# A gated delta rule inside a hybrid decoder trunk: the decay's running sums along the row, read from DRAM on every partition instead of made by broadcast products

## The chip, the core and the metric

The kernel runs on one core of one Trainium2 chip. The metric is the device time of one execution in microseconds (us), and the time of a kernel is the median over its runs. Beside the times there is one profiled execution, in which the hardware profiler records each instruction of the core's engines: PE is TensorE (matrix products, PEld its weight loads), DVE is VectorE, ACT is ScalarE, POOL is GpSimd, and SP issues DMAs. L121 means line 121 of the kernel. Each engine takes its own instructions strictly in the order in which they stand in its program; between engines they wait for one another by semaphores.

## What is computed

Two layers of a decoder trunk on 1024 tokens with model width 1024, all in float32. A layer normalises its input, makes one wide input projection from it, runs three token mixers side by side (a gated delta rule with 4 heads of width 128, latent attention with 8 heads, and a linear recurrence, RG-LRU, 512 wide), and adds one output projection to its input. The change lies in the delta rule, which works on chunks of 64 tokens:

```python
gc = jnp.cumsum(g.reshape(B, N, C, H).transpose(0, 1, 3, 2), axis=-1)   # g: log decay
decay = jnp.exp(jnp.where(tril, gc[..., :, None] - gc[..., None, :], -jnp.inf))
kbeta = kc * bc
a_mat = jnp.where(strict, jnp.einsum('bnhid,bnhjd->bnhij', kbeta, kc) * decay, 0.0) \
    + jnp.eye(C, dtype=q.dtype)
rhs = jnp.concatenate([vc * bc, kbeta * jnp.exp(gc)[..., None]], axis=-1)
sol = lax.linalg.triangular_solve(a_mat, rhs, left_side=True, lower=True, unit_diagonal=True)
attn = jnp.where(tril, jnp.einsum('bnhid,bnhjd->bnhij', qc, kc) * decay, 0.0)
```

For each chunk and head, `decay[i, j]` is the exponential of gc of token i minus gc of token j. One of the two varies down the partitions of a tile and can be a scalar per partition; the other varies along the row and must be there on every partition. This second one is what the change is about.

## The kernel before

**Tiling.** Tokens are taken in 8 units of 128 (two chunks each), and heads in two pairs. A quad is 2 units by 2 heads of a pair, that is four 128x128 blocks side by side in one tile of 128x512. There are four quads to a pair and 16 in the whole program (4 quads, 2 pairs, 2 layers).

**The stage around the change.** `phase_a` runs once a layer:

1. `gates` makes the log decay g [128 tokens, 32 columns (unit, head)], and from it with small products (L247, L249) the running sums `gs` by token, and their totals by chunk.
2. `gdn_qkv` makes q, k and v of pair 0.
3. For each pair: `gdn_tok` transposes k and v to rows of tokens (copies ktok and vtok), takes the squared norms of k by 16 squares on ACT into the tile sk (the squares themselves go to junk, L86), and from them rk (Ln, then Exp, with a table load before each), and on DVE the factors br and nbr2 and others.
4. `gdn_pre` for the four quads, the function that is changed. For each quad: products of the broadcast column of g with the constant upper triangle (L347, four of them) put the running sums along the row into a PSUM bank on every partition; DVE subtracts the per-token sums from them and adds a mask, for ea and et, four instructions each; ACT takes their exponentials; the k product (L360, four) gives k k^T, from which DVE makes a with nbr2 and ea, which goes to DRAM (L364); the q product (L367, four) gives k q^T, from which DVE makes at with et.
5. `gdn_inverse` for the pair, then `gdn_prep` and `gdn_scan` for each quad, then `gdn_norm`.

After both pairs come the RG-LRU, the output projection and the attention (`phase_c`).

**What fills in.** The input projection is made one column tile of 128 columns at a time: `in_tile` makes each in three float32r products per block of 128 rows (`mm3`, L121 to L123), into the PSUM tile pbig. `load_w` gets the weights: DMA to wst (L104), a rounded part whi by DVE (L111), the rest wlo by POOL (L112). Column tiles that the delta rule does not need itself are placed between its steps: one after `gdn_tok`, and in pair 0 another after each quad of `gdn_pre`.

**What sets the order.** A scheduler lays out each engine's instructions once, when the program is made, by priority and its expected durations. Projections have a much lower priority, by `LOW`, so a projection is placed where the scheduler expects PE to have nothing else that is ready. On the chip nothing is reordered.

**Buffers.** `bank("pr")` is a PSUM tag with two banks, taken in turn by the transposes, the products of L347, L360 and L367 and others; a product that takes a bank must wait until the earlier content was read. The tile ea has one buffer, et has one, a two, at four.

Of the kernel before, what the change touches and what calls it, by code (L numbers as in the profile page):

```python
# [15 lines left out]
T = 1024  # L16
# [6 lines left out]
# Columns of a layer's parameter tile [128, NPAR].  # L23
# [15 lines left out]
# Columns of the constant tile [128, NCON].  # L39
# [10 lines left out]
# Indices of the input projection's column tiles.  # L50
# [13 lines left out]
class Trunk:  # L64
# [7 lines left out]
    @contextmanager  # L72
    def prio(self, d):
        """Instructions that the scheduler prefers less (d > 0) or more (d < 0)."""
        self.tc.cur_priority += d
        yield
        self.tc.cur_priority -= d
# [19 lines left out]
    def load_w(self, src, nk, cols, eng=None, pool=None):  # L97
        """A float32 weight block [128, nk, cols] as its exact float32r parts."""
        nc = self.nc
        n = nk * cols  # L100
        wn = self.wn if pool is None else n
        pool = pool or self.pw
        st = pool.tile([128, wn], F32, name="wst", tag="wst")
        nc.sync.dma_start(st[:, :n], src.rearrange("p k c -> p (k c)"))  # L104
        hi = pool.tile([128, wn], F32R, name="whi", tag="whi")
        lo = pool.tile([128, wn], F32R, name="wlo", tag="wlo")
        with self.prio(-self.LOW):
            if wn <= 512:
                nc.scalar.copy(hi[:, :n], st[:, :n])  # L109
            else:  # L110
                nc.vector.tensor_copy(hi[:, :n], st[:, :n])  # L111
            (eng or nc.gpsimd).tensor_tensor(lo[:, :n], st[:, :n], hi[:, :n].bitcast(F32), ALU.subtract)  # L112
        return (hi[:, :n].rearrange("p (k c) -> p k c", k=nk),
                lo[:, :n].rearrange("p (k c) -> p k c", k=nk))

    def mm3(self, out, pairs):
        """out = sum over (ah, al, bh, bl) of a.T @ b, each in three float32r products."""
        nc = self.nc
        n = len(pairs)
        for j, (ah, al, bh, bl) in enumerate(pairs):  # L120
            nc.tensor.matmul(out, ah, bh, start=(j == 0), stop=False)  # L121
            nc.tensor.matmul(out, ah, bl, start=False, stop=False)  # L122
            nc.tensor.matmul(out, al, bh, start=False, stop=(j == n - 1))  # L123

    def split(self, hi, lo, x, eng=None):
        """x as exact float32r parts: hi is x rounded, lo the rest."""
        self.nc.scalar.copy(hi, x)  # L127
        (eng or self.nc.vector).tensor_tensor(lo, x, hi.bitcast(F32), ALU.subtract)  # L128

# [1 line left out]
    def in_tile(self, l, *ms):  # L131
        """The first of the column tiles ms; the others wait for their call. All by halves of the tokens."""
        if ms[0] not in self.ready:
            tiles = []
            for m in ms:
                hi, lo = self.early.pop(m, None) or self.load_w(self.i["w_in"][l, m], 8, 128)
                self.ready[m] = self.big()
                tiles.append((hi, lo, self.ready[m]))
            with self.prio(self.LOW):
                for n in range(2):  # L140
                    s = slice(n * H2, (n + 1) * H2)
                    for hi, lo, p in tiles:
                        self.mm3(p[:, s], [(hi[:, k], lo[:, k], self.hh[k][:, s], self.hl[k][:, s]) for k in range(8)])
        return self.ready.pop(ms[0])

    def conv(self, y, p, w, bias=None):
        """Causal depthwise conv of width 4 along the free axis, from PSUM."""
        if bias is None:
            self.act(y, p, AF.Copy, scale=w[:, 3:4])
        else:  # L150
            self.act(y, p, AF.Identity, scale=w[:, 3:4], bias=bias)
        for d in (1, 2, 3):
            self.stt(y[:, d:], p[:, : T - d], w[:, 3 - d : 4 - d], y[:, d:], ALU.mult, ALU.add)

    def silu2(self, out, z):
        """out = 2 silu(z), as z (1 + tanh(z / 2))."""
# [7 lines left out]
    def newton(self, r, x):  # L164
        """One Newton step of r towards x ** -0.5; x is overwritten."""
# [5 lines left out]
    def add_squares(self, alloc, acc, x, eng):  # L171
        """acc + x * x (acc is None at first)"""
# [7 lines left out]
    def rms_bcast(self, alloc, accs, n, ch, tag, fine=False):  # L180
        """1 / sqrt(mean of squares + eps), on every partition, from the sum of accs over their channels."""
        nc = self.nc
        r = alloc("rb")
        if not fine:
            # brings Ln's table in while the sums are still under way
            self.act(self.dummy, accs[-1][:, 0:1], AF.Ln, bias=self.eps)
# [14 lines left out]
    def norm_half(self, alloc, xs, accs, n, gain, tag, share=False):  # L201
        """h = rmsnorm(x) for one half of the tokens, into self.hh, self.hl."""
# [12 lines left out]
    def gates(self, l):  # L215
# [16 lines left out]
        # beside them the RG-LRU's parameters  # L232
# [15 lines left out]
        for j, c in ((1, K_H0), (2, K_H1)):  # L248
            nc.tensor.matmul(pc[:, 32 * j : 32 * j + 32], con[:, c : c + 1].to_broadcast([128, 128]), gf, start=True, stop=True)  # L249
        gs = pa.tile([128, 96], F32, name="gs")  # L250
# [19 lines left out]
    def gdn_qkv(self, l, pr, kind, hd, P):  # L270
# [22 lines left out]
        # squared norms of q, columns (unit, head)  # L293
# [7 lines left out]
    def combos(self, q):  # L301
        """The four (unit, head) of quad q: index, unit, head of the pair, columns."""
        return [(c, 2 * q + c // 2, c % 2, slice(c * 128, c * 128 + 128)) for c in range(4)]

    def gdn_tok(self, pr, P):
        """k and v by token, and the pair's factors per token."""
# [14 lines left out]
        # inverse norms: 1 / sqrt(sum + eps), of vectors that are twice the reference's  # L321
# [9 lines left out]
        # v is held doubled  # L331
# [7 lines left out]
    def gdn_pre(self, pr, P, q):  # L339
        """-A and the decayed attention of one quad; the diagonal blocks go out by DRAM."""  # L340
# [3 lines left out]
        pg = self.bank("pr")  # L344
        for c, u, hd, cs in self.combos(q):
            gj = u * 4 + 2 * pr + hd
            nc.tensor.matmul(pg[:, cs], self.g[:, gj : gj + 1].to_broadcast([128, 128]),  # L347
                             con[:, K_U : K_U + 128], start=True, stop=True)
# [23 lines left out]
    def blocks(self, dram, b):  # L372
        """Diagonal block b (32 x 32) of each of a pair's sixteen 128 x 128 matrices."""
        return bass.AP(dram.tensor, dram.offset + b * (32 * 2048 + 32), [[128, 16], [2048, 32], [1, 32]])

    def gdn_inverse(self, pr):
        """(I + A)^-1 of the 32 x 32 diagonal blocks, one block per partition, and its transpose."""
# [18 lines left out]
    def gdn_prep(self, pr, P, q):  # L396
        """The quad's triangular inverse, applied to v and k."""
# [29 lines left out]
        for hd in range(2):  # L427
            # w of a unit's two chunks around that unit's q
# [10 lines left out]
    def gdn_scan(self, pr, P, q):  # L439
# [6 lines left out]
        # the output takes the place of the decayed attention  # L446
# [30 lines left out]
    def gdn_norm(self, pr, P):  # L477
        """The output's RMS norm, its gate and its way out; q's inverse norm and 128^-0.5 with them."""
# [31 lines left out]
    def gate_tile(self, l, m, dst, z=None):  # L510
        """2 silu of a column tile, to DRAM"""
# [7 lines left out]
    def lru(self, l):  # L519
        nc, pa, par = self.nc, self.pa, self.par  # L520
        st, res = [], []
        for m in range(4):
# [22 lines left out]
            # 1 - a^2 = tanh(-log a) (1 + a^2)  # L545
# [112 lines left out]
    def rope(self, x, n, s):  # L658
        """Rotary embedding of one half of the tokens; x may be in PSUM."""
# [13 lines left out]
    def attn_q_rope(self, l, pr, res):  # L673
        """q's rotary part of two heads: parts stacked as [hi; lo] per head."""
# [30 lines left out]
    def attn_v(self, l, pr, V):  # L705
        """v of two heads: per two token blocks, [128, (block, head, 128)]."""
# [16 lines left out]
    def attn_scores(self, h, sb, q, qr, k, P):  # L723
        """The normalised probabilities of four query blocks."""
# [3 lines left out]
        for qi in range(4):  # L728
# [3 lines left out]
            # pieces of the keys, a PSUM bank each  # L732
# [34 lines left out]
            if qi == 3:  # L767
                # the transposes wait for the last block's first keys
# [9 lines left out]
    def attn_out(self, h, sb, P, V, ops):  # L778
        """Probabilities times v, gated; transposed a block of keys ahead of the product."""
# [56 lines left out]
    def out_proj_last(self, wsrc, ops, xin, xout, alloc):  # L836
        """The same by halves, with the sums kept on chip; yields each half's tiles and sums of squares."""
# [28 lines left out]
    def build(self):  # L866
# [5 lines left out]
        with sb("pk") as pk, sb("pg") as self.pg, sb("pf", 2) as self.pf, sb("ph", 16) as self.ph, \  # L872
# [14 lines left out]
            self.krd = dr("krd", 64)  # L887
            self.dz = [dr(f"dz{p}", 128, 2048) for p in range(2)]
# [23 lines left out]
    def first_norm(self, p0):  # L912
        """Loads x and the constants; the first layer's normalised input."""
# [92 lines left out]
    def phase_c(self, l, xd):  # L1006
# [19 lines left out]
        # Pieces of work by the time of their emission; a step is a head's half of the queries.  # L1026
# [85 lines left out]
def kblocks(w, nk, cols):  # L1112
    """[L, nk * 128, M * cols] as [L, M, 128, nk, cols]"""
# [63 lines left out]
```

## Time and profile before

| What | before |
| --- | --- |
| median of 3 runs | 2239.93 us (2239.56, 2239.93, 2247.45) |
| profiled execution, from its first to its last instruction (its span; no other time of it is given) | 2240.5 us |
| instructions in it | 28710 |
| bytes moved by DMA | 222.06 MB, 99 GB/s on the mean |
| the four stretches with `gdn_pre` | 136.9 to 162.2, 333.3 to 357.4, 1236.8 to 1262.0, 1437.6 to 1463.0 us |
| granted TensorE clock, mean of the span and in these four | 0.984; 1.00, 1.00, 1.00, 0.93 |

How to read it: a share of busy time is an average over stages with different limits. In a list by time a row has the start in us, the duration in us, the engine, the line, the operation, and "out<-in" by the names of the tiles, then partitions x elements; xN is the number of records, and what stands in square brackets is how long the engine was idle before it and what it waited for. One float32 128x128 product is two records. Matrix products run pipelined, so that the next one starts before the recorded end of the one ahead; the step from start to start is what one costs. The granted clock is the share of TensorE's full speed that the chip's throttle grants at that time.

### The profile page before, as it was taken

To read this page: it belongs to the slowest core of one execution; us is meant where nothing else is said; L and a number is where in the kernel's file an instruction comes from. 1 tells how busy PE (TensorE), PEld (TensorE's weight loads), DVE (VectorE), ACT (ScalarE), POOL (GpSimd) and SP (SyncE) were. 2 spreads that over 40 slices of the span, in tenths; PEclk is the share of its full clock that TensorE was granted. 3 is DMA by queue.
4 is the path that set the end of the run, shared out by engine and by line. 5 is a ranking of instruction groups with operands and counts; after the bars stand their busy time and mean duration, and the time that the engine had idled before them with its cause. 6 is when DMAs were issued, how large, how long until landed. Compare 5 with 4: busy or idle time off the path is not lost. (4 is left out here: it accounts for less than half of the span.)

```text
span 2240.5 us, 28710 instructions
## 1 busy us (share of the span) xinstructions
PE 2143.5 (96%) x10380; PEld 1695.7 (76%) x10380; DVE 1321.0 (59%) x2496; ACT 880.7 (39%) x1784; POOL 705.6 (31%) x712
## 2 busy tenths in 40 slices
PE   7999999999899999999989999999998999999997
PEld 4788877787677777777668888788777877777774
DVE  6546547545833766666664575483467247666666
ACT  5241254135611544443533313522375025443535
POOL 3222222323632333232242222322336323232322
PEclk9999999999999999999999999999999999999999
DMA  4223113412253024326321331134213520325172
GB/s 149 71 78 111 53 57 99 135 41 85 94 186 100 20 79 143 122 88 198 129 78 38 109 97 36 57 99 128 72 60 122 169 82 30 121 88 175 43 226 99
DMA packets 135101, 222.06 MB, mean 99 GB/s; under 512 B 37808, under 2 KB 60336, under 8 KB 134960
## 3 DMA queue, kind: packets, MB, share of 16 engines
q1 hardware_dynamic: 134960, 220.24, 30.6%
q8 instruction: 82, 1.34, 0.3%
q14 instruction: 59, 0.48, 0.1%
HBM read 147.31 MB, written 72.88 MB: 98 GB/s over the span
## 5 line engine op out<-in xcount | busy, mean ns | idle before, releaser
L112 POOL TENSOR_TENSOR wlo<-wst,whi 128x1024 fp32r<-128x1024 f32 (+3 forms) x196 | 316.2, 1614 | 903.6 <-DVE whi L111 308.8
L121 PE MATMUL pbig<-h,whi 128*128 128x512 f32 x1216 | 486.4, 400 | 9.2 <-ACT h L127 6.2
L123 PE MATMUL pbig<-h,wlo 128*128 128x512 f32 x1216 | 486.5, 400 | 4.0 <-POOL wlo L112 4.0
L122 PE MATMUL pbig<-h,whi 128*128 128x512 f32 x1216 | 485.8, 399 | 2.1 <-DVE h L128 1.0
L121 PEld LDWEIGHTS pbig<-h,whi 128*128 128x128 f32 x1216 | 231.7, 191 | 56.6 <-ACT h L127 7.0
L123 PEld LDWEIGHTS pbig<-h,wlo 128*128 128x128 f32 x1216 | 231.7, 191 | 50.8 <-POOL wlo L112 5.3
L122 PEld LDWEIGHTS pbig<-h,whi 128*128 128x128 f32 x1216 | 231.4, 190 | 50.2 <-POOL h L128 3.3
L86 ACT ACTIVATE P<-pS,mx,scq 128x512 f32<-128x512 f32 (+1 forms) x192 | 128.1, 671 | 158.9 <-DVE mx L89 88.2
L111 DVE CAST whi<-wst 128x1024 fp32r<-128x1024 f32 x92 | 76.9, 836 | 150.2 <-PE pbig L122 118.4
L95 POOL TENSOR_SCALAR P<-P,mx 128x128 f32<-128x128 f32 (+6 forms) x112 | 80.6, 720 | 231.0 <-DVE mx L766 186.9
L109 ACT CAST whi<-wst 128x256 fp32r<-128x256 f32 (+2 forms) x104 | 46.3, 447 | 231.3 <-DMA wst<-in_w_uq 105.2
L127 ACT CAST pth<-pstp 128x512 fp32r<-128x512 f32 x192 | 91.3, 479 | 93.2 <-PE pstp L795 93.2
L755 DVE TENSOR_REDUCE mx<-pS 128x1 f32<-128x512 f32 (+1 forms) x192 | 106.6, 555 | 24.3 <-PE pS L749 17.1
L128 DVE TENSOR_TENSOR ptl<-pstp,pth 128x512 fp32r<-128x512 f32 x192 | 105.1, 554 | 23.9 <-ACT pth L127 23.2
L86 ACT ACT_TABLE_LOAD x81 | 103.9, 1283 | 2.4 <-PEq L1169 0.7
L795 PE MATMUL pstp<-con,P 128*128 128x128 f32 x576 | 98.7, 278 | 3.4 <-DVE P L770 3.4
L121 PE MATMUL pspj<-lh,whi 128*128 128x512 f32 x208 | 88.1, 424 | 6.1 <-DVE k L128 5.5
L92 DVE TENSOR_TENSOR xt<-pspj,xt 128x512 f32<-128x512 f32 x96 | 66.3, 690 | 46.7 <-PE pspj L123 40.8
L795 PEld LDWEIGHTS pstp<-con,P 128*128 128x128 f32 x576 | 71.2, 141 | 25.0 <-DVE P L770 4.8
L749 PE MATMUL pS<-kl,qr 64*128 64x512 f32 (+1 forms) x192 | 85.1, 443 | 0.0
L123 PE MATMUL pspj<-lh,wlo 128*128 128x512 f32 x208 | 82.4, 396 | 0.6 <-POOL wlo L112 0.6
L122 PE MATMUL pspj<-ll,whi 128*128 128x512 f32 x208 | 82.4, 396 | 0.0
(267 smaller groups left out, 4565.5 us busy)
## 6 DMA issues: line engine op xcount, KB each, us to landing
wst<-in_w_in SPq DMA_DIRECT2D x76, 512.0 KB, 3.6
x<-xt SPq DMA_DIRECT2D x128, 256.0 KB, 3.2
xt<-x SPq DMA_DIRECT2D x112, 256.0 KB, 3.4
mzd<-z SPq DMA_DIRECT2D x16, 512.0 KB, 3.6
wst<-in_w_o SPq DMA_DIRECT2D x16, 512.0 KB, 3.6
mz<-mzd SPq DMA_DIRECT2D x32, 256.0 KB, 2.8
wst<-in_w_o SPq DMA_DIRECT2D x64, 128.0 KB, 2.1
xk<-x SPq DMA_DIRECT2D x32, 256.0 KB, 4.3
```

The costliest lines, as they stand in the source:

```text
L86: self.nc.scalar.activation(out, in_, func, **kw)
L95: self.nc.gpsimd.tensor_scalar(out, a, s, 1.0, ALU.mult, ALU.mult)
L111: nc.vector.tensor_copy(hi[:, :n], st[:, :n])
L112: (eng or nc.gpsimd).tensor_tensor(lo[:, :n], st[:, :n], hi[:, :n].bitcast(F32), ALU.subtract)
L121: nc.tensor.matmul(out, ah, bh, start=(j == 0), stop=False)
L122: nc.tensor.matmul(out, ah, bl, start=False, stop=False)
L123: nc.tensor.matmul(out, al, bh, start=False, stop=(j == n - 1))
L127: self.nc.scalar.copy(hi, x)
L128: (eng or self.nc.vector).tensor_tensor(lo, x, hi.bitcast(F32), ALU.subtract)
L749: nc.tensor.matmul(out, qr[sb][0:64, qs], self.kl[0:64, a:e], start=False, stop=True)
L755: nc.vector.tensor_reduce(mx[:, j : j + 1], S[j], AX.X, ALU.max, negate=True)
L795: nc.tensor.transpose(tp[:, qi * 128 : qi * 128 + 128], P[qi][:, kb * 128 : kb * 128 + 128], self.ident)
```

## The change

The running sums along the row are now made once a layer. In `gates` one more product makes all of them transposed, 32 rows (unit, head) of 128 tokens; ACT copies them to SBUF (`grow`), and a DMA writes them to a new DRAM tile `gcd`. In `gdn_pre` a DMA on SP's queue reads two rows of 256 values with a partition step of zero, so that all 128 partitions get them, into a new SBUF tile `gb` (128x512, two buffers), and DVE's eight instructions for ea and et read this tile instead of the PSUM bank. The four broadcast products of a quad are gone, and with them one use of the two PSUM banks per quad. The rest of the diff takes comments out, which moves later lines: the k product is now L363, the write of a L367, the q product L370.

```diff
@@ gates
     for j, c in ((1, K_H0), (2, K_H1)):
         nc.tensor.matmul(pc[:, 32 * j : 32 * j + 32], con[:, c : c + 1].to_broadcast([128, 128]), gf, start=True, stop=True)
+        nc.tensor.matmul(pc[0:32, 128:256], gf, con[:, K_U : K_U + 128], start=True, stop=True)
+        grow = self.pa.tile([32, 128], F32, name="grow")
+        nc.scalar.copy(grow, pc[0:32, 128:256])
+        nc.sync.dma_start(self.gcd, grow)
@@ gdn_pre
     et = pa.tile([128, H2], F32, name="et", tag="w2", bufs=1)
-        pg = self.bank("pr")
-        for c, u, hd, cs in self.combos(q):
-            gj = u * 4 + 2 * pr + hd
-            nc.tensor.matmul(pg[:, cs], self.g[:, gj : gj + 1].to_broadcast([128, 128]),
-                             con[:, K_U : K_U + 128], start=True, stop=True)
+        pg = pa.tile([128, H2], F32, name="gb", tag="gb", bufs=2)
+        rows = self.gcd[8 * q + 2 * pr : 8 * q + 2 * pr + 1]
+        nc.sync.dma_start(pg, bass.AP(rows.tensor, rows.offset, [[0, 128], [4 * 128, 2], [1, 256]]))
     for c, u, hd, cs in self.combos(q):
         gj = u * 4 + 2 * pr + hd
         self.stt(ea[:, cs], pg[:, cs], self.gc[:, gj : gj + 1], con[:, K_MA : K_MA + 128], ALU.subtract, ALU.add)
@@ build
         self.krd = dr("krd", 64)
+        self.gcd = dr("gcd", 32, 128)
```

Since the scheduler makes its order anew, the change also moves instructions that it does not touch. Three places show it, all in pair 0 of layer 0.

**PE, from the q product of quad 0 on.** pspr is a bank of the tag "pr", pbig the projections' tile; xN at the end of a row is N instructions one behind the other. Before, with the k product of quad 0 nine projections further up:

```order
L367 MATMUL pspr<-wq,kT 128x128 x4
L121 MATMUL pbig<-h,whi 128x512
L122 MATMUL pbig<-h,whi 128x512
L123 MATMUL pbig<-h,wlo 128x512
L121 MATMUL pbig<-h,whi 128x512
L347 MATMUL pspr<-con,g 128x128 x4
L122 MATMUL pbig<-h,whi 128x512
```

After, from the k product of quad 0 on:

```order
L363 MATMUL pspr<-kT 128x128 x4
L370 MATMUL pspr<-wq,kT 128x128 x4
L121 MATMUL pbig<-h,whi 128x512
L122 MATMUL pbig<-h,whi 128x512
L123 MATMUL pbig<-h,wlo 128x512
L121 MATMUL pbig<-h,whi 128x512
L363 MATMUL pspr<-kT 128x128 x4
L122 MATMUL pbig<-h,whi 128x512
```

Before, nine projections stood between quad 0's k product and its q product, and nine more between quad 1's broadcast products (the L347 shown) and its k product; now the q product follows the k product of quad 0 at once, and quad 1's k product comes after four projections. Behind it stand 19 projections, quad 1's q product, four, quad 2's k product, two, its q product, and 24 more. In pair 1 the order before was L347, L360, nine projections, L367, four, L347, four, L360; now it is L363, L370, four, L363, 16, L370, four, L363. Layer 1 has the same order as layer 0.

**ACT, at the end of the squares of k.** sk and rk are the tiles of the norms; one row is one instruction or a run of equal ones. Before:

```order
L86 ACTIVATE junk,sk<-ktok 128x128 x5
L86 ACTIVATE ea<-ea 128x512
L86 ACTIVATE junk,sk<-ktok 128x128 x2
L86 ACTIVATE et<-et 128x512
L86 ACTIVATE junk,sk<-ktok 128x128
L86 ACT_TABLE_LOAD
L86 ACTIVATE rk<-sk,ep 128x16
```

After:

```order
L86 ACTIVATE junk,sk<-ktok 128x128 x8
L86 ACT_TABLE_LOAD
L86 ACTIVATE rk<-sk,ep 128x16
L86 ACT_TABLE_LOAD
L86 ACTIVATE et<-et 128x512
L86 ACTIVATE rk<-rk 128x16
```

Quad 0's two exponentials have moved out from between the squares to a place far ahead of them; quad 1's exponential of et now stands between the second table load and rk.

**DVE, around a of quad 0.** nbr_943 and nbr_948 are the factor nbr2, gs the running sums by token, con the masks. Before:

```order
L89 SCALAR_TENSOR_TENSOR a<-pspr,nbr_943,ea 128x128 x4
L89 SCALAR_TENSOR_TENSOR ea<-pspr,gs,con 128x128 x4
L89 SCALAR_TENSOR_TENSOR et<-pspr,gs,con 128x128 x4
L89 SCALAR_TENSOR_TENSOR a<-pspr,nbr_943,ea 128x128
L111 CAST whi<-wst 128x1024
```

After:

```order
L89 SCALAR_TENSOR_TENSOR et<-gb,gs,con 128x128 x4
L92 TENSOR_TENSOR br<-rk,beta 128x16
L89 SCALAR_TENSOR_TENSOR nbr_948<-br,rk 128x16
L89 SCALAR_TENSOR_TENSOR br2e<-nbr_948,ge 128x16
L337 TENSOR_SCALAR br<-br 128x16
L89 SCALAR_TENSOR_TENSOR a<-pspr,nbr_948,ea 128x128 x4
L89 SCALAR_TENSOR_TENSOR ea<-gb,gs,con 128x128 x4
L92 TENSOR_TENSOR at<-pspr,et 128x512
L89 SCALAR_TENSOR_TENSOR a<-pspr,nbr_948,ea 128x128 x4
```

Before, quad 0's a was followed by ea and et of quad 1 and then by a and at of quad 1; now et of quad 1 stands ahead of the factors, and quad 1's at ahead of its a.

On SP's queue of the first layer the write of `gcd` stands between two weight loads, and the first three reads into gb stand, after one more weight load, ahead of the next six weight loads. Quad 0's ea and et of pair 0 are made while k of pair 0 still comes out of the projection.

## The prediction

> **What bounds the kernel now.** I read the page first (busy shares), then the waits of the matrix engine (PE), then PE, ACT and DVE in order of time where the edited function works, and last the granted clock there.
>
> ```profile
> span 2240.5 us, 28710 instructions
> PE 2143.5 (96%) x10380; PEld 1695.7 (76%) x10380; DVE 1321.0 (59%) x2496; ACT 880.7 (39%) x1784; POOL 705.6 (31%) x712
> ```
> PE is busy 96% of the span and no other engine reaches 60%: time goes where PE's time goes, and PE stands still for only some 97 us. So two things count, PE work taken away and PE waits made or removed. The second row below is from PE's waits, the first from the instructions that touch the tile g.
>
> ```profile
> L347 PE MATMUL pspr<-con,g x128: 270/275/377, 136.9 to 1459.3; 128*128 128x128 f32 x128
> PE pspr L360 <- DVE a L89: 5.6, 4, 2.2
> ```
> The products that go (L347) are 128 records for 64 calls, two a call. And of PE's waits, four, 5.6 us together, are in this very function: the second quad's k product (L360) waits for a on DVE. There are four because a pair of heads comes twice in each of two layers; I call the quads of a pair 0 to 3. This is pair 1 of layer 0 on PE:
>
> ```profile
> 333.32 1.16 PE L347 MATMUL pspr<-con,g 128*128 128x128 f32 x8
> 334.31 1.06 PE L360 MATMUL pspr<-kT 128*128 128x128 f32 x8
> ...
> 339.21 1.16 PE L347 MATMUL pspr<-con,g 128*128 128x128 f32 x8
> ...
> 340.90 0.40 PE L122 MATMUL pbig<-h,whi 128*128 128x512 f32 x1
> 343.52 1.16 PE L360 MATMUL pspr<-kT 128*128 128x128 f32 x8 [2.22 <-DVE a L89]
> 344.43 0.48 PE L123 MATMUL pbig<-h,wlo 128*128 128x512 f32 x1
> 344.75 0.40 PE L121 MATMUL pbig<-h,whi 128*128 128x512 f32 x1
> 344.98 0.39 PE L122 MATMUL pbig<-h,whi 128*128 128x512 f32 x1
> ...
> 346.35 1.06 PE L367 MATMUL pspr<-wq,kT 128*128 128x128 f32 x8
> 347.16 0.48 PE L122 MATMUL pbig<-h,whi 128*128 128x512 f32 x1
> ...
> 347.71 1.06 PE L347 MATMUL pspr<-con,g 128*128 128x128 f32 x8
> 348.60 1.06 PE L360 MATMUL pspr<-kT 128*128 128x128 f32 x8
> ```
> Between 334.31 and 343.52 PE has one k product, nine projections, the q product, four projections, one broadcast product and four projections, and still runs dry: the last projection starts at 340.90, the next slot would be 341.13 (projections follow each other by 0.23, as 344.75 and 344.98 do; the first behind another kind takes 0.32), and PE starts again at 343.52. That is 2.39 us from slot to slot. What it waits for is at the end of a chain on ACT:
>
> ```profile
> 335.24 0.31 ACT L86 ACTIVATE junk<-ktok 128x128 f32<-128x128 f32 x1
> ...
> 335.68 0.31 ACT L86 ACTIVATE junk<-ktok 128x128 f32<-128x128 f32 x1
> ...
> 335.99 0.62 ACT L86 ACTIVATE ea<-ea 128x512 f32<-128x512 f32 x1
> 336.51 0.29 ACT L86 ACTIVATE junk<-ktok 128x128 f32<-128x128 f32 x1
> ...
> 338.59 1.28 ACT L86 ACT_TABLE_LOAD   x1
> ...
> 341.50 0.21 ACT L86 ACTIVATE rk<-rk 128x16 f32<-128x16 f32 x1
> ```
> Sixteen squares (junk) give k's norms, then come a table load, Ln, a second table load and Exp (rk), and only then can DVE make nbr and a:
>
> ```profile
> 342.34 1.12 DVE L89 SCALAR_TENSOR_TENSOR a<-pspr,nbr,ea 128x128 f32<-128x128 f32 x4
> ...
> 347.55 0.69 DVE L92 TENSOR_TENSOR at<-pspr,et 128x512 f32<-128x512 f32 x1 [0.79 <-PE pspr L367]
> 348.15 0.68 DVE L111 CAST whi<-wst 128x1024 fp32r<-128x1024 f32 x1
> ```
> The chain does not depend on the broadcast. It ends when it ends, and PE needs work until then.
>
> **The change, part by part.** *Products removed.* 347.71 to 348.60 is 0.89 us for one quad's four products, 333.32 to 334.31 is 0.99 with a short wait in it. 16 quads x 0.90 = **14.4 us** of PE time (bounds 14.2 to 15.8), all of it on the engine that sets the end.
>
> *Products added.* One 32-row product a layer, two records as one of the four in L347: about 0.22. **+0.5 us** for both layers (0.1 to 1).
>
> *The order on PE.* Quad 0 now has k product, q product, four projections, and then the k product of quad 1. That product takes the PSUM bank of quad 0's k product (two banks, used in turn), so it must wait until DVE has read it for a, just as now. But nine projections, a broadcast and four (pair 1) or nine (pair 0) more projections no longer stand ahead of it. In pair 1 the k product starts at 333.32, where the first broadcast was; two products (0.89, and 0.81 as from 346.35 to 347.16) and four projections (0.32 + 3 x 0.23 = 1.01) leave PE free at 336.03. The chain on ACT is shorter by one exponential: with ea between them two squares are 0.83 apart (335.68 to 336.51), otherwise 0.44 (335.24 to 335.68), so 0.4 is won; et's place is taken by quad 1's et. So a ends at 343.06 and PE resumes at 343.12: a wait of **7.1 us** instead of 2.39. Pair 0 likewise:
>
> ```profile
> 136.90 1.05 PE L347 MATMUL pspr<-con,g 128*128 128x128 f32 x8
> ...
> 145.52 0.40 PE L121 MATMUL pbig<-h,whi 128*128 128x512 f32 x1
> 146.49 1.16 PE L360 MATMUL pspr<-kT 128*128 128x128 f32 x8 [0.57 <-DVE a L89]
> ```
> PE is free at 136.90 + 2.71 = 139.61. Two exponentials leave ACT's chain (-0.8), but quad 1's et now stands between the second table load and rk (+0.5): PE resumes at 146.2, a wait of **6.6 us** instead of 0.74. Layer 1 has the same order and waits (the four of the row above). Extra: 2 x (7.1 + 6.6) - 2 x (2.39 + 0.74) = **+21.1 us** (19 to 23).
>
> *A second wait.* Quad 1's a now stands behind its at on DVE. In the rows, at starts 1.20 after its product (346.35 to 347.55), the next instruction follows 0.60 later, and a takes 1.12: a is done 2.92 us after the q product starts. PE is ready for quad 2's k product after 0.81 + 1.01 = 1.82. A wait of 1.1 us, four times: **+4.4** (2 to 6).
>
> *The clock.* One of the four old waits, in layer 1, shows what follows a wait:
>
> ```profile
> 1447.78 2.08 PE L360 MATMUL pspr<-kT 128*128 128x128 f32 x8 [2.19 <-DVE a L89]
> ...
> 1452.17 1.06 PE L367 MATMUL pspr<-wq,kT 128*128 128x128 f32 x8
> 1449.00:1451.00 2.00, 2.00 (x9) 1.71 (x8) 2.00 (x8) 1.25 (x2) 0.51 (x2) 0.50 0.13 49
> ```
> (The last row is the stretch from 1449 to 1451; the granted clock is its third figure from the right.) It fell to 0.50, and the k product with the same eight projections took 4.39 us instead of the 2.83 of layer 0 (343.52 to 346.35): 1.56 us lost. In layer 0 the wait of 2.22 us cost nothing. Waits three times as long should each cost about that: 4 x 1.56, less the one paid now, **+4.7** (0 to +10.9, the latter if each costs double). [...]
>
> *Loads.* A row write and eight 256 KB loads a layer, all on SP. The nearest prices:
>
> ```profile
> dn<-a SPq DMA_DIRECT2D x16, 256.0 KB, 2.3
> x<-in_x SPq DMA_DIRECT2D x16, 256.0 KB, 5.6
> L249 PE MATMUL pspr<-g,con x8: 276/324/403, 59.2 to 1158.1; 128*128 128x32 f32 x8
> 72.80 62.59 SPq L104 DMA_DIRECT2D wst<-in_w_in  x6
> 64.19 1.23 DVE L89 SCALAR_TENSOR_TENSOR kT<-th,kT 128x1024 f32<-128x1024 f32 x1 [1.19 <-ACT th L86]
> 69.54 0.69 DVE L111 CAST whi<-wst 128x1024 fp32r<-128x1024 f32 x1 [4.12 <-PE pbig L122]
> ```
> In pair 0 the first load's readers stand ahead of a kT instruction on DVE, hence also of the cast at 69.54 and the weights behind it. Two DMAs of 2.3 to 5.6 us after a product behind L249 (59.2) bring the row at 64 to 71; DVE is idle 4.12 us there, and the cast's weights are two column tiles ahead of PE. On SP the third load waits for quad 0's et ahead of six weight loads, whose first went out at 72.80 before, later than that et. I take **0** (0 to 3, if a load lands near 75).
>
> *DVE's 128 instructions that read gb from SBUF instead of PSUM* (eight a quad). Their length stays about 0.34, but they may now be held up by POOL:
>
> ```profile
> 201.92 2.42 DVE L92 TENSOR_TENSOR itmp<-inv 64x150 f32<-64x150 f32 x1
> ...
> 205.39 0.30 DVE L92 TENSOR_TENSOR inv<-inv,itmp 64x150 f32<-64x150 f32 x1
> 201.78 2.39 POOL L112 TENSOR_TENSOR wlo<-wst,whi 128x1024 fp32r<-128x1024 f32 x1 [9.69 <-DVE whi L111]
> ```
> An instruction with two SBUF tensors takes 2.42 us instead of 0.30 when POOL is in its wlo. In each pair one wlo falls among quad 2's et; PE has 19 to 24 projections (4.4 to 5.5 us) as cover there, so I charge 0.2 a pair, **+0.8** (0 to 8.4, a full 2.1 four times).
>
> The sum: 2240.5 - 14.4 + 0.5 + 21.1 + 4.4 + 4.7 + 0.8 = 2257.6. The median of the runs shown (2239.93) is 0.6 below the profiled span, so the forecast is **2257.0 us**, slower by 0.8%. A measurement of this kernel can tell about 0.5% (11.2 us) from no change.
>
> **The rivals.** *The removed work counts in full (faster).* If a of quad 0 were ready when PE asks, the time would be 2240.5 - 14.4 + 0.5 - 0.6 = 2226. It decides at a shorter chain: all extra waiting must stay under 14 us, so a would have to end about 3 us earlier in each pair than I walked it, more than both table loads (2.56) together. For it: PE's order is made from expected durations in which this order was the better one. Against it: the squares and table loads are ACT's own work, and only 0.3 to 0.4 us of it leaves. 8%.
>
> *The waits come, the clock holds.* Then 2252.3 or, with each wait a little shorter than walked, 2240 to 2251: within 0.5%. The 2.22 us wait without loss speaks for it, the length of the new waits against it. 14%.
>
> *POOL decides.* With all 16 quads held up 2.1 us on the path: 2257 + 16 x 2.1 = 2291; with one a pair 2265. [...] Against it: in this function POOL mostly runs instructions of 0.37 us. Above 2267: 6%.
>
> *The loads arrive late*, so that the change trades a product for a DMA wait: DVE would show waits for gb, at 2 to 5 us each. Queue order and cover speak against it; it is inside the 6%.
>
> **How the numbers follow.** The forecast's own case (2247 to 2267) holds 72%, of which the part below 2251 is counted as no change. The low end is the sum with the smallest waits and no clock loss (2252 - 5), the high end adds double clock loss and a little of POOL (2257 + 6 + 4). With the rivals: faster by over 0.5% 0.08, within 0.5% 0.17, slower by over 0.5% 0.75.
>
> **What would show it.** Right: PE's waits have "pspr L363 <- DVE a" eight times, four of 6 to 7 us and four near 1 us, some 30 us in all; the granted clock is 0.50 just after the four long ones; ACT's chain to rk has the same two table loads; gb never appears as what DVE waits for on the path. Wrong: if these waits stay under 3 us, or if DVE's ea and et take over 1 us each, or if PE waits in another stage.

## The result and the profile after

| | before | after |
| --- | --- | --- |
| median of 6 runs each | 2239.91 us | 2252.59 us |
| ratio, 95% interval | | 1.0056 [1.0036, 1.0075] |
| span of the profiled execution | 2240.5 us | 2250.9 us |

The changed kernel is slower by 12.7 us, 0.56%. The time forecast was 2257.0, with a range of 2247 to 2267. The 0.56% lies just above the 0.5% that the prediction took as its line, and the interval reaches to both sides of that line. The number says little about the reasons: some of the terms were wrong, in both directions. First the page of the changed kernel, its span and busy times:

```profile
span 2250.9 us, 28478 instructions
PE 2137.7 (95%) x10256; PEld 1682.4 (75%) x10256; DVE 1339.6 (60%) x2496; ACT 879.1 (39%) x1784; POOL 707.8 (31%) x712
```

128 records of broadcast products are gone from PE, four of the new product have come, and PE is busy 5.8 us less, yet the span is longer by 10.4. DVE, with as many instructions as before, is busy 18.6 us more. So PE waits more, and DVE's instructions take longer. Which ones, the groups of DVE's instructions show (number, busy us, mean ns of one, idle time before them):

```profile
L89 DVE SCALAR_TENSOR_TENSOR et<-gb,gs,con 128x128 f32<-128x128 f32 x64 | 27.2, 478 | 1.8 <-PE pspr L437 1.6
L89 DVE SCALAR_TENSOR_TENSOR ea<-gb,gs,con 128x128 f32<-128x128 f32 x64 | 24.9, 442 | 4.8 <-DMA gb<-gcd 4.6
```

The same 128 instructions took 18.2 and 17.9 us before, 344 and 342 ns each; they account for 16.0 of the 18.6 us. PE's waits with the delta rule's tiles, by what ended them (us, how often, the longest):

```profile
PE pspr L370 <- DVE a L89: 6.7, 4, 2.2
PE pspr L363 <- DVE a L89: 5.7, 4, 2.4
...
PE pspr L499 <- POOL at L95: 3.6, 2, 1.8
PE pspr L429 <- DVE tf L92: 3.5, 2, 1.7
...
PE pspr L363 <- DVE at L92: 0.5, 3, 0.2
```

Before, the one wait of PE for a was that of the k product, 5.6 us. Now it waits 12.4 us for a in two places, and in addition for tf (a step of `gdn_prep`) and at (in `gdn_norm`). All waits that the trace prints on PE's rows sum to 98.3 us, against 82.1 before.

**The first place is not the one forecast.** Pair 0 of layer 0 on PE and DVE, in order of time:

```profile
138.60 1.05 PE L363 MATMUL pspr<-kT 128*128 128x128 f32 x8
139.49 1.06 PE L370 MATMUL pspr<-wq,kT 128*128 128x128 f32 x8
...
141.33 1.16 PE L363 MATMUL pspr<-kT 128*128 128x128 f32 x8
...
147.95 1.16 PE L370 MATMUL pspr<-wq,kT 128*128 128x128 f32 x8 [1.13 <-DVE a L89]
140.58 0.69 DVE L92 TENSOR_TENSOR at<-pspr,et 128x512 f32<-128x512 f32 x1 [5.29 <-PE pspr L370]
...
146.78 1.12 DVE L89 SCALAR_TENSOR_TENSOR a<-pspr,nbr,ea 128x128 f32<-128x128 f32 x4
```

Quad 1's k product starts at 141.33, when DVE is through with at of quad 0 (140.58 + 0.69) and five microseconds before it starts on a of quad 0. So it does not take the bank of quad 0's k product: it takes that of quad 0's q product, which is read early. The two banks are not taken in turn here. It is quad 1's q product that needs the other bank and waits for a, and between the two products stand 19 projections that cover the time: the wait is 1.13 us, not 6.6.

**The second place was forecast as nearly nothing.** Pair 1 of layer 0 (PE, DVE, POOL):

```profile
344.58 1.16 PE L370 MATMUL pspr<-wq,kT 128*128 128x128 f32 x8 [2.22 <-DVE a L89]
...
356.12 1.86 PE L363 MATMUL pspr<-kT 128*128 128x128 f32 x8 [2.44 <-DVE a L89]
349.90 5.13 DVE L89 SCALAR_TENSOR_TENSOR et<-gb,gs,con 128x128 f32<-128x128 f32 x3
354.95 1.11 DVE L89 SCALAR_TENSOR_TENSOR a<-pspr,nbr,ea 128x128 f32<-128x128 f32 x4
349.73 2.52 POOL L112 TENSOR_TENSOR wlo<-wst,whi 128x1024 fp32r<-128x1024 f32 x1 [3.31 <-DVE ea L89]
352.21 2.41 POOL L177 TENSOR_TENSOR sq<-sq 128x1024 f32<-128x1024 f32 x1
```

Three instructions of et take 5.13 us, where the three of ea just ahead of them (at 349.11) take 0.87, and POOL is meanwhile in its wlo and, straight behind it, in the latents' sum of squares (sq). The first two of the three, one by one:

```profile
349.90 2.50 DVE L89 SCALAR_TENSOR_TENSOR et<-gb,gs,con 128x128 f32<-128x128 f32 x1
352.32 2.45 DVE L89 SCALAR_TENSOR_TENSOR et<-gb,gs,con 128x128 f32<-128x128 f32 x1
```

Each ends 0.15 us after one of POOL's two instructions; the third takes 0.34. So each of these two instructions of POOL holds up one of DVE's. Behind them a is late, and PE waits 2.44 us. In the kernel before, the same two POOL instructions stood beside the same work:

```profile
349.85 1.12 DVE L89 SCALAR_TENSOR_TENSOR et<-pspr,gs,con 128x128 f32<-128x128 f32 x4
349.07 2.40 POOL L112 TENSOR_TENSOR wlo<-wst,whi 128x1024 fp32r<-128x1024 f32 x1 [3.83 <-DVE whi L111]
351.44 2.36 POOL L177 TENSOR_TENSOR sq<-sq 128x1024 f32<-128x1024 f32 x1
```

There et read PSUM, and four took 1.12 us beside POOL's 2.40 and 2.36.

**Where the time went.** The projections moved within a pair's part of the stage, but from the first k product of pair 0 to that of pair 1 as many are done after as before (579 a layer), and so from the first k product of pair 1 to the output projection (843). So these two stretches can be compared. The clock blurs them: in these two traces the granted clock falls to 0.50 in stretches of 3.41, 6.83 or 10.24 us (and at the very end), not all at the same places: in pair 1's quads from 356.39 and 1455.48 in the changed kernel, from 1447.70 alone in the kernel before. This is the one behind the wait of 2.44 us above (busy times of PE, PEld, DVE, ACT, POOL, then granted clock, DMA share, GB/s):

```profile
356.40:359.80 3.40, 3.40 (x17) 3.40 (x17) 3.40 (x13) 1.56 (x3) 0.00 (x0) 0.50 0.23 82
```

In such a stretch projections follow each other by 0.43 us instead of 0.23 (those at 60.67 and 61.10 for instance), and half of PE's busy time, 1.7 us here, is lost. Over the whole execution that is 28.5 us before and 32.7 us after. But 4.6 and 1.7 us of these fall ahead of the first product of `gates` (L247), which starts at 59.0 and 58.8 us all the same, so that nothing is lost there. Behind it the loss is 23.9 and 31.0 us: of the 10.4 us between the spans some 7.1 are the clock's, and 3.3 are left.

These are two executions. The mean granted clock is on record for every run of the experiments and of the changed kernel: the time multiplied by (1 - clock) is 42.4 us for the changed kernel (mean of six runs) and 36.1 us for the kernel before (mean of 75), and over these 75 runs the time rises by 0.81 us for each us of it. By this estimate some 5 of the 12.7 us are the clock's.

The table takes half of PE's busy time at 0.50 off the stretches of both layers together (last column: how much was taken off). It is worked out from the starts of PE's instructions in each trace, and three kernels with PE's order of before (the first three rows) stand in it as a measure of its scatter. In pair 1 e9 also has PE's order of before, and e10 that of the changed kernel:

| us, both layers | pair 0 | pair 1 | taken off |
| --- | --- | --- | --- |
| before | 394.3 | 540.5 | 8.2 |
| additions alone (e1) | 393.3 | 540.8 | 8.5 |
| one tensor operand, before (e3) | 393.9 | 540.2 | 11.9 |
| after | 388.8 | 547.2 | 11.9 |
| one tensor operand, after (e2) | 392.1 | 545.1 | 8.5 |
| pair 0 changed alone (e9) | 390.8 | 541.1 | 6.8 |
| pair 1 changed alone (e10) | 391.8 | 545.6 | 11.9 |
| quad 2 of pair 1 unchanged (e11) | 388.3 | 541.2 | 10.1 |
| sq on DVE, after (e5) | 388.7 | 537.2 | 6.8 |
| sq on DVE, before (e6) | 393.4 | 541.9 | 11.9 |

The change gains 5.5 us in pair 0 and loses 6.7 in pair 1. The broadcast products of a pair's first quad stand ahead of its first k product. So pair 0's stretch had the products of four quads a layer taken away, three of its own and those of pair 1's first (7.2 us in both layers), and pair 1's stretch those of three (5.4 us). Pair 1's stretch thus takes on some 12 us, and the waits printed on PE's rows in it rise from 16.2 to 27.6 us. For the same reason pair 0's stretch has one quad's products a layer more in e9 than after, and one fewer in e10 than before. Counted from the first product of `gates` on, with the clock left out, another 2 us come in the rest of the program, where the code is otherwise the same.

### The profile page after: what moved, and what is told of

Same layout as the page of the kernel before. It is cut to its first block, busy times and chain, and to the rows that moved or that the text cites. A ratio compares the mean times of both kernels' runs of the same rounds, so it can differ in the third digit from the quotient of the medians.

```text
span 2250.9 us, 28478 instructions
## 1 busy us (share of the span) xinstructions
PE 2137.7 (95%) x10256; PEld 1682.4 (75%) x10256; DVE 1339.6 (60%) x2496; ACT 879.1 (39%) x1784; POOL 707.8 (31%) x712
## 5 line engine op out<-in xcount | busy, mean ns | idle before, releaser
L128 DVE TENSOR_TENSOR ptl<-pstp,pth 128x512 fp32r<-128x512 f32 x192 | 105.1, 554 | 23.9 <-ACT pth L127 23.3
L86 ACT ACTIVATE z<-pbig 128x1024 f32<-128x1024 f32 x24 | 24.5, 1022 | 155.6 <-PE pbig L123 134.1
```

The costliest lines, as they stand in the source:

```text
L86: self.nc.scalar.activation(out, in_, func, **kw)
```

## The experiments

All were timed in five rounds beside the kernel before, but for e3 with three. Each of the groups e1 to e4, e5 to e8 and e9 to e11 shares its runs of the kernel before, whose medians were 2242.48, 2244.07 and 2242.32 us.

**e1: the additions alone.**

```diff
@@ before, gates
+        nc.tensor.matmul(pc[0:32, 128:256], gf, con[:, K_U : K_U + 128], start=True, stop=True)
+        grow = self.pa.tile([32, 128], F32, name="grow")
+        nc.scalar.copy(grow, pc[0:32, 128:256])
+        nc.sync.dma_start(self.gcd, grow)
...
@@ before, build
+            self.gcd = dr("gcd", 32, 128)
```

> The kernel before with the change's additions in gates alone (32-row product, copy, write of gcd); nothing reads gcd, the broadcast products stay, and every engine's order around the quads is that of before. If the new work in gates and on SP's queue carries the loss, +5 to +12 us (2245 to 2252). If the loss lies in the quads and behind them (order of the projections, or DVE held up by POOL), only the products' own 1.1 us and no more than another 1 us: 2240 to 2242.

Measured: 2245.34 us, ratio 1.0018 [1.0002, 1.0035]: 0.4 to 7.8 us. The interval reaches into both expectations. In the trace the pairs' stretches are those of before to within 1 us (table), and the quads of pair 0 take 24.4 us in both layers as before. From the first product of `gates` to the first k product, where the additions stand, e1 takes 78.9 and 79.3 us in the two layers, halved clock taken off, and the kernel before 78.8 and 78.7. The new product is the only thing that is added on PE:

```profile
L251 PE MATMUL pspr<-con,g x4: 421/422/422, 59.5 to 1170.4; 128*32 128x128 f32 x4
```

(this line is of the changed kernel: number of records, shortest, median and longest in ns; in both layers the granted clock was 0.50 there). So by the trace the additions cost about one microsecond and are not what makes the change lose; the times alone leave up to 7.8 us open.

**e2 and e3: one tensor operand.** Each of ea and et becomes

```diff
-            self.stt(et[:, cs], pg[:, cs], self.gc[:, gj : gj + 1], con[:, K_MT : K_MT + 128], ALU.subtract, ALU.add)
+            nc.vector.tensor_scalar(et[:, cs], pg[:, cs], self.gc[:, gj : gj + 1], 0.0, ALU.subtract, ALU.min)
```

in the changed kernel (e2) and in the one before (e3); the line shown is that of et, and ea has `ALU.max` in place of `ALU.min`. The causal masks of both are left out.

> The changed kernel, with ea and et made by an instruction with one tensor operand (gb minus the scalar, clamped at 0) instead of two; the masks are left out. PE's order in the four quad stretches is that of the changed kernel. Theory contention (DVE reading two SBUF tensors is shut out while POOL works on wlo and sq): no ea or et instruction takes over 1 us, the wait of quad 3's k product in pair 1 (2.44 us in layer 0 of the changed kernel) goes, and the time falls by 5 to 9 us, to 2244 to 2248. Theory order (where the projections stand): the wait stays above 1.5 us and the time stays at 2250 to 2254.

> Control for the run above: the kernel before with the same instruction with one tensor operand, reading PSUM; masks left out, order of all engines as before. Both theories: 2238 to 2241, no change. If it is faster by over 4 us, the shorter instruction itself helps, and the run above proves nothing about contention.

Measured: e2 2252.28 us, 1.0044 [1.0027, 1.0062]; e3 2245.05 us, 1.0006 [0.9989, 1.0023]. The control shows no change, as expected; that its time lies above 2241 goes with the 2242.48 of the kernel before beside it. In e2 the hold-up stayed (list of DVE):

```profile
350.24 5.14 DVE L354 TENSOR_SCALAR ea<-gb,gs 128x128 f32<-128x128 f32 x4
355.30 0.67 DVE L358 TENSOR_SCALAR et<-gb,gs 128x128 f32<-128x128 f32 x3
```

The experiment rested on an assumption that is wrong: that one tensor from SBUF cannot be held up. It is: the four instructions of ea, which read one float32 tensor, took 5.14 us together, where the next quad's four (at 357.78) took 0.86. The longest of ea in this run took 2.43 us, against a median of 0.28, so at least two of the four were held up; POOL's wlo waits for a reader of gb there as in the changed kernel (6.4 us in two waits, 7.8 there). By itself the run decides nothing between the theories; e11 below gives it something to be compared with.

**e4: gb by way of PSUM.**

```diff
+        gb = pg
+        pg = self.bank("pr")
+        nc.scalar.copy(pg, gb)
```

> The changed kernel, with gb copied by ACT into a bank of the tag pr, from which DVE reads as in the kernel before: no DVE instruction reads gb from SBUF, each quad uses three banks again, and 11, 13, 7, 7 projections stand between k and q products in pair 0. If what costs is contention and too few projections ahead of waiting products, both are gone, and the removed products count: 2240 - 14 + 1 = 2227, up to 2232 with waits for the 16 copies. If the removed products cannot pay whatever the order is (a later stage takes the time back), 2238 to 2252.

Measured: 2271.85 us, 1.0126 [1.0096, 1.0156], slower than both. Both expectations failed, the first by 40 us and the second by 20, though the conditions of the first were met: no DVE instruction reads gb, and in the quads of pair 1 only the wait for quad 0's a is left (2.3 us, against 2.2 in both other kernels). The longest waits are behind them on PE, 9.6 us in each layer:

```profile
388.38 0.80 PE L121 MATMUL pbig<-h,whi 128*128 128x512 f32 x1 [9.62 <-ACT sq L86]
```

The order made for this kernel puts 30 projections fewer between pair 1's quads and its prep. That the projections therefore run out of free PSUM tiles, while the latents' norm is still under way on DVE and ACT, is read from this trace and not tested. The copies and the other order cost more here than the whole change.

**e5 and e6: sq on DVE.** In `lat_q` and `lat_kv`, in the changed kernel (e5) and the one before (e6):

```diff
-                acc = self.add_squares(self.c4, acc, p, nc.gpsimd)
+                acc = self.add_squares(self.c4, acc, p, nc.vector)
```

> The changed kernel, with the latents' sums of squares (sq) done on DVE instead of POOL, so that POOL has one instruction of 2.4 us (wlo) beside pair 1's ea and et instead of two in a row. PE's order in the quads is that of the changed kernel but for three more projections ahead of quad 3. Theory contention: ea or et there is held up for 2.5 us instead of 5.1, the wait of quad 3's k product in pair 1 (2.44 and 1 to 2 us in the two layers) falls under 0.5 us, and the time falls by 3 to 5 us against the changed kernel, to 2248 to 2250. Theory order (DVE is held up but PE has cover): the wait falls by the 0.7 us of the three projections alone, and the time stays within 2 us of 2252.

> Control: the kernel before with the same move of sq to DVE; PE's order in the quads as before but for five more projections in quad 2 of pair 1. Theory contention: 2238 to 2243, since ea and et read PSUM and were not held up. If it gains as much as the run above, sq on POOL costs somewhere else.

Measured: e5 2238.82 us, 0.9979 [0.9964, 0.9994]; e6 2245.04 us, 1.0007 [0.9997, 1.0016]. The control does not move. With this one line the change loses nothing any more: e5 is faster than the kernel before and, by the ratios, than the changed kernel by 0.8%. DVE and POOL in e5:

```profile
351.83 3.02 DVE L89 SCALAR_TENSOR_TENSOR et<-gb,gs,con 128x128 f32<-128x128 f32 x3
354.78 1.21 DVE L177 TENSOR_TENSOR sq<-sq 128x1024 f32<-128x1024 f32 x1
351.67 2.51 POOL L112 TENSOR_TENSOR wlo<-wst,whi 128x1024 fp32r<-128x1024 f32 x1 [3.31 <-DVE ea L89]
```

With one POOL instruction beside it one instruction of et is held up instead of two, the three take 3.02 us instead of 5.13, and the longest wait of the k product falls from 2.4 to 0.8 us. That is a good deal less than the 10 us that pair 1 gains in the table, and the time, some 17 us below that of the changed kernel by the ratios, moved by more than three times the expected 3 to 5 us. Moving sq also gave another order behind the quads (the waits for tf are gone). e5 alone therefore does not say how much of the gain is the hold-up.

**e7 and e8: more projections in pair 1's quads.**

```diff
-    FILL = ((1, 1, 2, 0, 1), (1, 0, 3, 0, 2))
+    FILL = ((1, 1, 2, 0, 1), (1, 1, 2, 0, 2))
```

> The changed kernel with other column tiles between the quads of pair 1 (one after each quad, two instead of three after the inverse), so that 41 projections stand behind quad 0's q product and 24 ahead of quad 3's k product. Theory order (the removed products count where PE has cover): in pair 1 the waits of 2.2 and 2.4 us are gone, and against the control below, with the same tiles, this run is faster by 3 to 10 us. Theory that the removed work comes back as waits whatever the tiles: slower than the control by 5 to 12 us, as the change is with the tiles that it has.

> Control: the kernel before with the same column tiles between the quads of pair 1. PE has 32 projections and more ahead of quad 1's k product, so its wait of 2.2 us goes; what the other stages make of it is not known: 2235 to 2255.

Measured: e7 2288.81 us, 1.0209 [1.0183, 1.0235]; e8 2288.90 us, 1.0202 [1.0186, 1.0219]. Neither theory's number came: with these tiles the change makes no difference. It was a poor test, since the tiles brought the latents' norm among the quads, and PE waits there for other things, in e7 for instance

```profile
350.62 3.72 PE L191 MATMUL pspr<-sq,ep 128*128 128x512 f32 x4 [5.58 <-POOL sq L177]
```

It shows that the change is worth +0.56%, -0.3% (e5 against e6) or nothing according to what else stands at that place.

**e9 and e10: the two halves.** Pair `(pr, q)` decides where the row comes from:

```diff
+        if (pr, q) in BY_PRODUCT:
+            pg = self.bank("pr")
...
+        else:
             pg = pa.tile([128, H2], F32, name="gb", tag="gb", bufs=2)
```

with the quads of pair 1 by product in e9, those of pair 0 in e10.

> Half the change: pair 0's quads read gb, pair 1's quads have their broadcast products in PSUM as before. PE's order in pair 0 is that of the changed kernel, in pair 1 and behind it that of before. Theory pair 1 (the change gains in pair 0, where it took 2.6 us off the quads, and loses in pair 1, where DVE is held up beside POOL's wlo and sq and the scan has fewer projections): faster than before by 3 to 6 us. Theory that the loss is spread over both pairs or comes from the loads: slower than before by 2 to 7 us, half of the change's 12.7.

> The other half: pair 0's quads have their broadcast products, pair 1's read gb. PE's order in pair 0 is that of before, in pair 1 and behind it that of the changed kernel. Theory pair 1: slower than before by 11 to 18 us, more than the whole change. Theory spread: slower by 5 to 8 us.

Measured: e9 2245.27 us, 1.0002 [0.9984, 1.0020]; e10 2258.04 us, 1.0072 [1.0044, 1.0100]. Pair 1 alone costs 16 us (10 to 22 by the interval), as the theory of pair 1 has it and as much as the whole change within the intervals; the 5 to 8 us of the other theory lie outside. Some 7 of the 16 are the clock's by the estimate above (45.2 us on the mean of e10's runs against 36.1). For pair 0 alone the expected 3 to 6 us did not come: the interval, 3.6 us faster to 4.5 slower, holds only the smallest of them. In the trace pair 0 of e9 gains 3.5 us (390.8 against 394.3), from which the additions go off.

**e11: one quad left as before**, quad 2 of pair 1 by product, all others from gb.

> The changed kernel with broadcast products in quad 2 of pair 1 alone, the quad whose et was held up for 5.1 us beside POOL's wlo and sq. Theory contention: ea and et of that quad take 1.1 us for four again, quad 3's k product waits under 0.5 us instead of 2.4, and the stretch of the quads of pair 1 is shorter than that of the changed kernel by 1 to 2 us in each layer, the added products (0.9 us each) counted; the whole, with the new order behind it, 2240 to 2250. If the hold-up was not what PE waited for, the wait stays above 1.5 us and the stretch gets 0.9 us longer.

Measured: 2242.52 us, 0.9996 [0.9980, 1.0012]. Putting back 1 of the 8 quads a layer takes away the whole loss, 0.6% by the ratios. DVE, then POOL:

```profile
350.07 1.12 DVE L89 SCALAR_TENSOR_TENSOR et<-pspr,gs,con 128x128 f32<-128x128 f32 x4
...
349.91 2.41 POOL L112 TENSOR_TENSOR wlo<-wst,whi 128x1024 fp32r<-128x1024 f32 x1 [4.45 <-DVE ea L89]
352.27 2.40 POOL L177 TENSOR_TENSOR sq<-sq 128x1024 f32<-128x1024 f32 x1
353.75 1.06 PE L370 MATMUL pspr<-kT 128*128 128x128 f32 x8
```

POOL does the same, et is not held up, and quad 3's k product (the last row) does not wait. From pair 1's first k product to its last q product, halved clock taken off, the two layers together take 40.6 us instead of the changed kernel's 45.9. The two sets of products put back (1.8 us) and eight projections that went elsewhere (8 x 0.23) cancel, so the 5.3 us are the hold-up's, against 2.44 and 2.42 us that PE waited there. That much of the loss is shown to come from DVE and POOL. Of the remaining gain in the span some 2 us are waits elsewhere, and 8.0 are the clock, which was halved for less of this execution (24.7 us lost instead of 32.7). But the profiled execution is the fastest of e11's twelve; by the mean of the runs (38.5 us against 42.4 by the measure above) the clock has some 3 us of the gain.

The one quad changes more than the hold-up: the order behind the quads is another too, and the waits for tf and at are gone. e2 separates the two. Behind quad 3 of pair 1 it has the order of e11 on PE, but for the place of two projections, and no wait for tf or at either; but it has the hold-up, and quad 3's k product waits 3.38 us. Its pair 1 takes 545.1 us and that of e11 541.2, with 1.8 us of products more, and its time is 0.44% above the kernel before where that of e11 is not. So the loss stays without the waits for tf and at, and in pair 1 it goes with the hold-up. (e2 is also slower than e11 by 3.8 us in pair 0, for which no run shows a reason.)

## Why the prediction was right, and where not

The direction and the time were right, and few of the terms that made the sum. By the signs that it named itself, its account was wrong: no wait for a reached 3 us in the changed kernel, two instructions of et took 2.5 us each in pair 1 of both layers, and PE waits in other stages.

- **Products removed, -14.4; product added, +0.5.** Held: 128 records went, and from start to start they had taken 14.5 us in the trace of before. The new product cost about twice what was said, some 1.1 us.
- **The order on PE, +21.1.** This step failed. It said "That product takes the PSUM bank of quad 0's k product (two banks, used in turn)". It took the bank of the q product instead, which was free early. The q product now waits for a, with 19 and 16 projections between the two: 6.7 us in four waits where the k product had waited 5.6. The term was about 1 us. The bank was taken from a rule on turns and not read off.
- **A second wait, +4.4.** It said that "Quad 1's a now stands behind its at on DVE", and that holds; but the bank that quad 2's k product takes is again the one that at has freed. The wait was 0.17 us.
- **DVE's reads from SBUF, +0.8 (0 to 8.4).** The mechanism was right, and mis-sized in its term: "PE has 19 to 24 projections (4.4 to 5.5 us) as cover there". In pair 1 POOL has two instructions in a row, as the rows of the kernel before show too, each of them holds up one et, and 5.13 us are longer than the cover, which left a wait of 2.4 us in each layer: 4.9 instead of 0.8. The rival "POOL decides" was given 6%; with this one quad put back (e11) the loss is gone.
- **The clock, +4.7.** The size fits, with some 5 us by the mean of the runs and 7.1 between the two profiled executions. The place does not: of the four long waits that it was put on none exists, and in pair 1's quads the halved stretches begin at 356.39 and 1455.48 in the changed kernel, at 1447.70 alone in the one before. Of the six runs of the changed kernel the slowest, 2260.55 us, had a mean granted clock of 0.979, and the fastest, 2247.62 us, of 0.985.
- **Stages behind the quads, nothing.** The forecast left them out. In pair 1 of both layers 23 projections fewer stand between the first prep and the norm, and PE waits there for tf (3.5 us) and at (3.6 us). The kernels with 130 projections there (before, e1, e3, e9, e2 and e11) have neither wait, with the hold-up (e2) or without it; the changed kernel and e10, with 107, have both; e5 and e6, with 105 and 112, wait for at alone (2.2 and 1.3 us). This speaks for the order as their cause; no run changes the order alone.
- **Additions and loads.** Taken as 0 to 3, and held: no row has PE waiting for gb. DVE waited for it 4.6 us (the second row of the groups above).

So the forecast was right by luck, by two errors that met: some 24 us of waits for a that did not come, and some 15 us of other waits, of which it had 0.8 (the 10.4 us between the spans, plus 14.4 for the products, less 1.1 for the new one, 1.6 for the waits for a and at that did come, and 7.1 for the clock). 12 us of these have a name: 4.9 behind the held-up et, 3.5 for tf, 3.6 for at. The faster rival's condition, that a be ready when PE asks, was met more nearly than thought; the time did not follow because of the hold-up of DVE by POOL, the waits behind the quads and the clock.

The version that is faster than both is e5: the change together with sq on DVE, 0.2% below the kernel before. What stays open is why the time of e9 shows nothing of what pair 0 gains in its trace, and some 3.6 us of the span from the output projection to the attention, which have the same code and other waits (the three kernels with PE's order of before differ there by up to 1.6 us).

## What to carry to other kernels

Moving an operand from PSUM to SBUF changed more here than where it is read: three instructions took 5.13 us instead of 0.87 beside two of POOL's. So for each DVE instruction that reads it, look which POOL instructions run beside it, how many of them in a row, and whether PE's cover is longer than that. Before a wait is put on a reused buffer, read off which buffer is taken and who reads it last; "in turn" is a guess. And where a scheduler fills gaps, removed work is first of all a new order: test the parts with the order of the rest held fixed, as the two halves by pair of heads did here for pair 1.

## What was not expected of the hardware

Beside et of quad 2 in pair 1, which read gb from SBUF, POOL's wlo and sq held up one DVE instruction each: beside two of 2.52 and 2.41 us in a row, two of et took 2.50 and 2.45 and the third 0.34; beside a single one of 2.51 the three of et took 3.02 together (e5). The first of the two ended 0.15 us after POOL's first (352.39 and 352.24); the second, which started 0.11 us after POOL's second (352.32 and 352.21), ended 0.15 us after that one (354.77 and 354.62). Instructions with a single float32 tensor from SBUF (e2) took up to 2.43 us, against a median of 0.28. With the first tensor in PSUM, four of the same instructions took 1.12 us beside the same POOL work (e11).
